# A one-core hybrid backbone (retention, then gMLP): sums of weight quarters recorded one item ahead, and one product moved to another PSUM tag

## The chip, the cores and the metric

The kernel runs on one core of a Trainium2 chip. The metric is the device time of one execution in microseconds (us), lower is better. Engines by the names of the profile: PE (TensorE, the matmuls), PEld (its weight loads), DVE (VectorE), ACT (ScalarE), POOL (GpSimd), SP (SyncE, which here issues most of the DMA loads).

## The reference

Two layers over 512 latent tokens of width 1024, with 256 context tokens ahead of them. Layer 0 mixes tokens by bidirectional multi-scale retention, layer 1 by a chunked gMLP. Cut to what matters here:

```python
for i in range(DEPTH):                                   # 2 layers
    shift_x, scale_x, gate_x = jnp.split(silu_c @ ada_w[i] + ada_b[i], 3, axis=-1)
    hx = rmsnorm(x, norm_g[i]) * (1 + scale_x[:, None]) + shift_x[:, None]
    ...
    if kind == 0:   # q, k, v, z = hx @ w_in (and hc for the context), retention, @ w_out
        out_x, out_c = retention_mixer(hx, hc, ret_w_in[j], ret_decay[j], ret_w_out[j], need_ctx)
    elif kind == 1: # u, v, z = hx @ w_in, norm of v, mix within chunks of 128 tokens, gate, @ w_out
        out_x = gmlp_chunk_mixer(hx, gm_w_in[j], gm_vnorm_g[j], gm_w_s[j], gm_b_s[j], gm_w_out[j])
    x = x + gate_x[:, None] * out_x
return rmsnorm(x, final_g)
```

All data are 32-bit floats. `rmsnorm` needs one inverse root for each token.

## The kernel before

**Products of quarters.** A product with a weight matrix is made quad by quad: a quad is a 2 x 2 block of the weights, with raw quarters 11, 12, 21, 22, each 128 x 1024 numbers in an SBUF slot. Instead of eight quarter products it makes seven, on sums of quarters and of activations (lines 150 to 153): T1 = 12 − 11, T2 = 22 − T1's sum, T3 = 22 − 12, T4 = 21 − T2's sum, each formed in place of a raw quarter, beside the plain B11, B21, B22. The activations' counterparts are A11, A12, A22 and S1 to S4 (in the profile oA and oS). `PAIRED` and `SINGLE` give the order of the seven.

**Halves.** TensorE multiplies numbers of reduced mantissa here, so every operand is split into a high and a low half, and a product is three matmuls (`mm3`, line 125). `split` (line 132) does it for the weights: ACT casts the item to its high half, then DVE subtracts that from the item to get the low half. Both lie in one `hl` tile; four hl tiles rotate. So an item costs ACT a cast, and DVE a low half and, for a T item, a sum ahead of it.

**The stream.** Class `Stream` (line 155) holds the list of items, in the order in which TensorE takes them. `get` returns the next item's tile and calls `upto`, which keeps two items ahead: for each it records the sum (T items; for the last weights a product with the gate in its place), then `split`, then gives the raw slots back (`drop`), after which `pump` issues the next loads on SP.

**Banks.** PSUM has eight banks here: six of tag "ps", two of tag "tm" (`pt`, line 121). Class `Product` (line 329) takes x from "ps" (B11, T2, T3 and T4 accumulate there) and y and z from "tm". ACT copies a bank to SBUF (`snap`), DVE adds a bank to such a copy (`plus`, in the profile `snap<-pst,snap`); T4 goes on in bank x after DVE's plus for T3 has read it.

**Layer 1's norm.** At the end of layer 0 `by_tokens` transposes the residual stream into banks, ACT squares and sums them there, and `residual` (line 1099) copies the same banks to `xs` tiles on ACT, which POOL's queue spills to DRAM. `inverse` forms the inverse roots, `rms` (line 1113) spreads them over the partitions by a product with the unit matrix, two matmuls into a bank, which ACT copies to `rs`. `second_half` (line 1147) is called step by step between the first products of layer 1 and makes the S and A operands from rs.

**Order.** TensorE's instructions stay in the order in which they are recorded. Those of ACT and DVE (and with them the loads on SP and spills on POOL) are put in order by a scheduler when the kernel is built; after that the order on each engine is fixed. It works from the order of recording and from its own estimates of what is ready. All instructions are recorded through one helper, so the profile has line 54 for each.

Of the kernel before, what the change touches and what calls it, by code (L numbers as in the profile page):

```python
# [10 lines left out]
ALU = mybir.AluOpType  # L11
AX = mybir.AxisListType

P = 128
# [12 lines left out]
HS = 256  # L27
# [40 lines left out]
def hybrid_kernel(ctx, tc, xT_d, cT_d, cv_d, sv_d, rows_d, ada0_d, adag_d, w_d, rope_d, dec_d, ws_d, id_d, out_d):  # L68
    nc = tc.nc
    pe, act, dve, sp = (Queue(tc, e) for e in (nc.tensor, nc.scalar, nc.vector, nc.sync))  # L70
# [11 lines left out]
    def st(shape, tag, dt=F32, bufs=1, name=None):  # L82
        return sb.tile(shape, dt, tag=tag, name=name or tag, bufs=bufs)
# [26 lines left out]
    def hl_tile(moves=False):  # L110

        i = hls[0] % HL
        hls[0] += 1
        t = st([P, 2080], f"hl{i}", F32R, name="hl")
        o = 32 if moves != (i % 2 == 1) else 0
        return t[:, o:o + 2048].rearrange("p (a n) -> p a n", a=2)
# [4 lines left out]
    def pt(shape=(P, 512), tag="ps"):  # L121
        return ps.tile(list(shape), F32, tag=tag, name="pst", bufs=6 if tag == "ps" else 2)
# [9 lines left out]
    def split(hl, src, late=None):  # L132
        h, l = hl
        act.copy(h, src)
        low = lambda: dve.tensor_tensor(l, src, f32(h), ALU.subtract)
        if late is None:
            low()
        else:
            late.append(low)
# [15 lines left out]
    class Stream:  # L155
# [3 lines left out]
        def __init__(self):  # L159
            self.items, self.loads, self.raws, self.left, self.tiles = [], [], {}, {}, {}  # L160
            self.free, self.stage, self.done, self.sent, self.at = [], 0, 0, 0, -1
            self.gate = self.limit = self.cap = None

        def quad(self, q, names, place=None):
            for name in names:
                self.item(q, name, place)
# [28 lines left out]
        def upto(self, n, late=None):  # L195

            while self.done < min(n, self.limit or len(self.items)):
                q, name, uses, at, place = self.items[self.done]
                self.pump()
                raw = lambda u: self.raws[q, u]  # L200
                r = raw(at)
                if name[0] == "T":
                    dve.tensor_tensor(r, raw(uses[0]), raw(uses[1]), ALU.subtract)
                elif name[0] == "gated":
                    g = self.gate[:, name[1]:name[1] + 512].unsqueeze(1).to_broadcast([P, 2, 512])
                    rr = r.rearrange("p (e n) -> p e n", e=2)
                    dve.tensor_tensor(rr, rr, g, ALU.mult)
                hl = place() if place else hl_tile(q[0] in ("vz", "v1"))
                split((hl[:, 0, :], hl[:, 1, :]), r, late)
                self.tiles[self.done] = hl  # L210
                self.done += 1
                if late is None:
                    self.drop(q, uses)
                else:
                    late.append(lambda: self.drop(q, uses))

        def drop(self, q, uses):
            for u in uses:
                e = self.left[q, u]
                e[1] -= 1  # L220
                if not e[1]:
                    self.free.append(e[0])
            self.pump()
# [349 lines left out]
    def project(q):  # L573
        if q[0] == "kq":
            return Product(features, kq_done(q[1]), hc)
        return Product(tokens, vz_done(q[1], q[2]), hc)
# [349 lines left out]
    for n, q in enumerate(QUADS[3:]):  # L926
        pr = project(q)
# [183 lines left out]
        dve.reciprocal(s[:, 1, :], s[:, 1, :])  # L1111

    def rms(hf):
        pr = pt((P, HS))
        for i in range(2):
            mm(pr[:, i * P:i * P + P], sums[hf][:, 1, i:i + 1].to_broadcast([P, P]), ident, start=True, stop=True)
        rs = st([P, HS], "rs1", name="rs1")
        act.copy(rs, pr)
        return rs.unsqueeze(1).to_broadcast([P, 4, HS])
# [7 lines left out]
    def first_half(hf, c):  # L1127
        if hf == 0:
            if c == 3:
                by_tokens(0, 0)  # L1130
            return
        if c == 0:
            by_tokens(0, 1)
            inverse(0)
        if c == 2:
            residual()
        if c == 3:
            by_tokens(1, 0)
        if c != 1:
            return  # L1140
        rb = rms(0)
        for g, q in ((0, "11"), (1, "12")):
            op("A" + q)
            scaled(quarter[q], 0, g, rb)
            keep("A" + q, quarter[q])

    def second_half():
        f11, f12, f21, v = (quarter[q] for q in ("11", "12", "21", "22"))
        by_tokens(1, 1)
        inverse(1)  # L1150
        yield
        rb = rms(1)
        dve.tensor_tensor(v, v, rb, ALU.mult)
        op("S1")
        for k in range(4):
            act.activation(A["S1"][:, 0, k, :], v[:, k, :], AF.Identity, bias=shs[:, k:k + 1])
            dve.scalar_tensor_tensor(A["S1"][:, 1, k, :], v[:, k, :], shs[:, k:k + 1], f32(A["S1"][:, 0, k, :]), ALU.add, ALU.subtract)
        yield
        for k in range(4):
            dve.scalar_tensor_tensor(v[:, k, :], v[:, k, :], shs[:, k:k + 1], f11[:, k, :], ALU.add, ALU.subtract)  # L1160
        op("S2")
        keep("S2", v)
        yield
        dve.tensor_tensor(f12, f12, v, ALU.subtract)
        op("S4")
        keep("S4", f12)
        scaled(f21, 1, 0, rb)
        yield
        dve.tensor_tensor(f21, f11, f21, ALU.subtract)
        op("S3")  # L1170
        keep("S3", f21)
        yield
        scaled(f11, 1, 1, rb)
        op("A22")
        keep("A22", f11)
        yield
# [302 lines left out]
```

## Time and profile before

| | us |
|---|---|
| times of three runs | 898.55, 896.89, 896.98 |
| median | 896.98 |
| profiled execution, its own time | 898.68 |
| span of the profiled execution | 896.9 |
| PE busy | 881.9 (98%) |
| DVE busy | 712.7 (79%) |
| ACT busy | 461.2 (51%) |
| POOL busy | 51.5 (6%) |
| DVE, 195 low halves | 236.9, 1.22 each |
| DVE, 92 sums of quarters | 111.5, 1.22 each |
| ACT, 195 casts | 203.6, 1.05 each |

Times within the execution count from the start of the span. Busy times of PE overlap by the pipelining of its matmuls, so a busy share of PE says only that it did not stand idle.

### The profile page before, as it was taken

How to read it: one execution, taken by the hardware profiler on the slowest of the kernel's cores; microseconds unless marked ns; L12 is line 12 of the kernel's file. 1: busy time of each engine (PE TensorE's matmuls, PEld its weight loads, DVE VectorE, ACT ScalarE, POOL GpSimd, SP SyncE). 2: the span in 40 equal slices, each digit the busy share in tenths (PEclk: the TensorE clock that was granted, in tenths of full speed). 3: DMA queues.
4: the chain of work that ended last, by engine and by line, in shares of the span. 5: the costliest groups of instructions: out<-in, count | busy, mean ns of one | idle time of the engine just before them, and what ended most of it. 6: DMA issues, size and time to landing. Idle time of an engine off the chain costs nothing.

```text
span 896.9 us, 16938 instructions
## 1 busy us (share of the span) xinstructions
PE 881.9 (98%) x6884; PEld 839.2 (94%) x6884; DVE 712.7 (79%) x996; ACT 461.2 (51%) x717; POOL 51.5 (6%) x88
## 2 busy tenths in 40 slices
PE   8999999999999999999999999999999999999997
PEld 7899999999999999998989999999999899899986
DVE  2689967699679877877678568999888578688995
ACT  5464644444355534636365438744666446356434
POOL 0001211001101101000000001010000000000000
PEclk9999999999999999999999999999999999999999
DMA  9933968457477448747445421545334235136212
GB/s 334 403 126 107 301 216 260 142 177 242 144 251 239 145 160 329 267 137 253 147 130 176 142 70 62 183 165 192 130 119 166 69 118 179 33 118 211 75 44 94
DMA packets 75486, 153.81 MB, mean 171 GB/s; under 512 B 7696, under 2 KB 34448, under 8 KB 75408
## 3 DMA queue, kind: packets, MB, share of 16 engines
q1 hardware_dynamic: 68544, 130.69, 44.0%
q0 software_dynamic: 6720, 22.03, 6.5%
q8 instruction: 54, 0.88, 0.4%
q14 instruction: 24, 0.20, 0.1%
q10 hardware_dynamic: 144, 0.01, 0.0%
HBM read 128.58 MB, written 24.12 MB: 170 GB/s over the span
## 4 chain that ended last, share of the span: by engine, by line
PE 88%; DVE 5%; ACT 3%; DMA 2%; issue 1%; SPq 1%; DVEq 0%; ACTq 0%
PE pst L54 88%; DVE hl L54 2%; DMA xq<-in_xT_dram 1%; DVE raw L54 1%; DMA raw<-in_w_dram 1%; ACT hl L54 1%; ACT junk L54 1%; SPq L54 1%; ACT f L54 1%; ACT oA L54 0%; DVE ada_a L54 0%; DVE pf L54 0%; DVE pl L54 0%; DVE o L54 0%; DVE f L54 0%
## 5 line engine op out<-in xcount | busy, mean ns | idle before, releaser
L54 DVE TENSOR_TENSOR hl<-raw,hl 128x1024 fp32r<-128x1024 f32 x195 | 236.9, 1222 | 79.4 <-ACT hl L54 79.2
L54 ACT CAST hl<-raw 128x1024 fp32r<-128x1024 f32 x195 | 203.6, 1050 | 140.0 <-PE pst L54 68.9
L54 PE MATMUL pst<-hl,oS 128*128 128x256 f32 x1152 | 138.6, 282 | 2.1 <-DVE hl L54 1.9
L54 PEld LDWEIGHTS pst<-hl,oS 128*128 128x128 f32 x1152 | 136.6, 190 | 3.4 <-DVE hl L54 2.1
L54 PE MATMUL pst<-oS,hl 128*128 128x256 f32 x1104 | 133.6, 280 | 0.7 <-ACT oS L54 0.5
L54 PEld LDWEIGHTS pst<-oS,hl 128*128 128x128 f32 x1104 | 130.2, 189 | 2.3 <-ACT oS L54 1.0
L54 PE MATMUL pst<-oA,hl 128*128 128x256 f32 x936 | 117.4, 281 | 0.2
L54 PEld LDWEIGHTS pst<-oA,hl 128*128 128x128 f32 x936 | 112.0, 189 | 2.5 <-issue 1.2
L54 DVE TENSOR_TENSOR raw<-raw 128x1024 f32<-128x1024 f32 x92 | 111.5, 1219 | 1.4 <-DMA raw<-in_w_dram 0.7
L54 ACT COPY snap<-pst 128x512 f32<-128x512 f32 x92 | 53.8, 585 | 104.1 <-PE pst L54 103.7
L54 PE MATMUL pst<-hl,oA 128*128 128x256 f32 x816 | 99.3, 280 | 0.0
L54 PEld LDWEIGHTS pst<-hl,oA 128*128 128x128 f32 x816 | 97.2, 189 | 0.1
L54 PE MATMUL pst<-og,hl 128*128 128x256 f32 x768 | 92.5, 281 | 0.0
L54 PEld LDWEIGHTS pst<-og,hl 128*128 128x128 f32 x768 | 90.4, 189 | 0.9 <-issue 0.2
L54 PE MATMUL pst<-v,ph 128*128 128x512 f32 x192 | 60.1, 395 | 0.0
L54 PE MATMUL pst<-hl,ya 128*128 128x512 f32 (+1 forms) x246 | 59.2, 386 | 0.0
L54 PEld LDWEIGHTS pst<-hl,ya 128*128 128x128 f32 x246 | 45.3, 188 | 9.5
L54 DVE TENSOR_TENSOR snap<-pst,snap 128x512 f32<-128x512 f32 x69 | 47.3, 686 | 5.3 <-PE pst L54 5.1
L54 ACT CAST ph<-pf 128x512 fp32r<-128x512 f32 x24 | 14.9, 621 | 67.3 <-DVE pf L54 66.9
L54 PE MATMUL pst<-hl,hc 128*128 128x256 f32 x384 | 47.1, 279 | 0.0
L54 PEld LDWEIGHTS pst<-hl,hc 128*128 128x128 f32 x384 | 45.6, 189 | 0.0
L54 PEld LDWEIGHTS pst<-v,ph 128*128 128x128 f32 x192 | 36.2, 188 | 7.3
(177 smaller groups left out, 1003.2 us busy)
## 6 DMA issues: line engine op xcount, KB each, us to landing
raw<-in_w_dram SPq DMA_DIRECT2D x224, 256.0 KB, 3.9
bg<-in_adag_dram SPq DMA_DIRECT2D x32, 512.0 KB, 4.3
ada_w<-in_ada_dram SPq DMA_DIRECT2D x16, 512.0 KB, 8.9
raw<-in_w_dram SPq DMA_DIRECT2D x16, 512.0 KB, 4.4
bg<-in_dec_dram SPq DMA_DIRECT2D x12, 512.0 KB, 4.3
v<-snap POOLq DMA_DIRECT2D x16, 256.0 KB, 4.9
z<-snap POOLq DMA_DIRECT2D x16, 256.0 KB, 3.8
v<-v SPq DMA_DIRECT2D x8, 512.0 KB, 4.2
```

The lines of the kernel that those rows point to most:

```text
L54: made = op(*args, **kw)
```

## The change

Two edits. The first takes the code that forms an item's sum out of `upto` into a method `sum`, which notes in `summed` that it was done. `upto` calls it for an item ahead of its split, as before, and after its loop once more, for the next item, if that item's raw quarters are loaded and it does not lie past the limit. So the sum of an item is recorded one item earlier than its split. The second edit takes the bank of `rms` from tag "tm" instead of "ps". Both kernels have the same instructions on every engine, in TensorE's case in the same order.

```diff
@@ upto
-                raw = lambda u: self.raws[q, u]
-                r = raw(at)
-                if name[0] == "T":
-                    dve.tensor_tensor(r, raw(uses[0]), raw(uses[1]), ALU.subtract)
-                elif name[0] == "gated":
-                    g = self.gate[:, name[1]:name[1] + 512].unsqueeze(1).to_broadcast([P, 2, 512])
-                    rr = r.rearrange("p (e n) -> p e n", e=2)
-                    dve.tensor_tensor(rr, rr, g, ALU.mult)
+                r = self.raws[q, at]
+                self.sum(self.done)
                 hl = place() if place else hl_tile(q[0] in ("vz", "v1"))
                 split((hl[:, 0, :], hl[:, 1, :]), r, late)
...
+            if self.limit is None or self.done < self.limit:
+                self.sum(self.done)
+
+        def sum(self, n):
+
+            if n >= len(self.items) or n in self.summed:
+                return
+            q, name, uses, at, place = self.items[n]
+            if name[0] not in ("T", "gated") or any((q, u) not in self.raws for u in uses):
+                return
+            self.summed.add(n)
...
@@ rms
-        pr = pt((P, HS))
+        pr = pt((P, HS), tag="tm")
```

**Where the order moves (1).** DVE in layer 0, the quad vz 2, 1 (about us 211 to 224 of the span). raw_2239 is quarter 11, later the sums of T1 and then T2; raw_2306 quarter 12, later T3; raw_2309 is 22, raw_2505 is 21, later T4. hl_2682 is T1's tile, hl_2716 T2's, hl_2772 B21's, hl_2803 T3's; a row hl<-raw,hl is a low half. Before:

```order
L54 TENSOR_TENSOR snap_2532<-pst_2464,snap_2532 128x512
L54 TENSOR_TENSOR rope_a_2671<-rope_a_2671,rope_b_2672 128x256 x2
L54 TENSOR_SCALAR ada_a_2299<-bg_2601,cpad_177,ada_a_2299 128x1024
L54 TENSOR_TENSOR raw_2239<-raw_2306,raw_2239 128x1024
L54 TENSOR_TENSOR raw_2306<-raw_2309,raw_2306 128x1024
L54 TENSOR_TENSOR hl_2772<-raw_2505,hl_2772 128x1024
L54 TENSOR_TENSOR hl_2682<-raw_2239,hl_2682 128x1024
L54 TENSOR_SCALAR ada_a_2299<-bg_2678,cpad_177,ada_a_2299 128x1024
L54 TENSOR_TENSOR raw_2239<-raw_2309,raw_2239 128x1024
L54 TENSOR_TENSOR hl_2803<-raw_2306,hl_2803 128x1024
L54 TENSOR_TENSOR raw_2505<-raw_2505,raw_2239 128x1024
L54 TENSOR_TENSOR hl_2716<-raw_2239,hl_2716 128x1024
```

The same place of the changed kernel (numbers of tiles that aren't quarters or hl shift by one):

```order
L54 TENSOR_TENSOR raw_2239<-raw_2306,raw_2239 128x1024
L54 TENSOR_TENSOR snap_2532<-pst_2465,snap_2532 128x512
L54 TENSOR_TENSOR rope_a_2672<-rope_a_2672,rope_b_2673 128x256 x2
L54 TENSOR_SCALAR ada_a_2300<-bg_2602,cpad_177,ada_a_2300 128x1024
L54 TENSOR_TENSOR hl_2682<-raw_2239,hl_2682 128x1024
L54 TENSOR_TENSOR hl_2772<-raw_2505,hl_2772 128x1024
L54 TENSOR_TENSOR raw_2239<-raw_2309,raw_2239 128x1024
L54 TENSOR_SCALAR ada_a_2300<-bg_2679,cpad_177,ada_a_2300 128x1024
L54 TENSOR_TENSOR hl_2716<-raw_2239,hl_2716 128x1024
```

T1's sum has moved ahead of the bank's drain, T2's low half follows its sum with one operation between, and T3's sum and low half and T4's sum, which stood ahead of T2's low half, come later.

**Where the order moves (2).** ACT at the start of layer 1 (about us 557 to 561). pst_6588 (6589 in the changed kernel) is the bank of `rms`. Before:

```order
L54 COPY snap_6586<-pst_6561 128x512
L54 COPY xs_6676<-pst_6471 128x512
L54 COPY xs_6679<-pst_6478 128x512
L54 COPY xs_6682<-pst_6543 128x512
L54 COPY rs1_6591<-pst_6588 128x256
L54 COPY xs_6685<-pst_6550 128x512
```

Now:

```order
L54 COPY snap_6587<-pst_6562 128x512
L54 COPY rs1_6592<-pst_6589 128x256
L54 COPY xs_6677<-pst_6472 128x512
L54 COPY xs_6680<-pst_6479 128x512
L54 COPY xs_6683<-pst_6544 128x512
L54 ACTIVATE oS1_6595<-f22_6141,shs_911,oS1_6595 128x256 x4
```

The copy of the inverse roots now stands ahead of three of the residual's copies instead of behind them.

**Where the order moves (3).** DVE in the same stage. The first two products of layer 1 run side by side (q = 0 and 1); raw_6218 becomes T4's sum of the one, raw_6221 of the other, raw_6212 and raw_6215 hold the T2 sums, hl_6906 and hl_6944 are T4's tiles of the two. Before, about us 556 to 562:

```order
L54 TENSOR_TENSOR raw_6212<-raw_6230,raw_6212 128x1024
L54 RECIPROCAL sums_6137<-sums_6137 128x2
L54 TENSOR_TENSOR raw_6215<-raw_6233,raw_6215 128x1024
L54 TENSOR_TENSOR raw_6218<-raw_6218,raw_6212 128x1024
L54 TENSOR_TENSOR raw_6221<-raw_6221,raw_6215 128x1024
L54 TENSOR_TENSOR f22_6141<-f22_6141,rs1_6591 128x1024
L54 TENSOR_TENSOR f21_6140<-acc_4217,rs1_6591 128x1024
```

In the changed kernel the two T4 sums stand some 25 rows later, shortly ahead of the low halves that need them:

```order
L54 BN_STATS bns_6516<-snap_6786 128x6 x2
L54 TENSOR_TENSOR raw_6218<-raw_6218,raw_6212 128x1024
L54 TENSOR_TENSOR oA22_6865<-f11_6138,oA22_6865 128x1024
L54 TENSOR_TENSOR snap_6820<-pst_6732,snap_6820 128x512
L54 TENSOR_TENSOR hl_6906<-raw_6218,hl_6906 128x1024
L54 BN_STATS bns_6516<-snap_6820 128x6 x2
L54 TENSOR_TENSOR raw_6221<-raw_6221,raw_6215 128x1024
L54 TENSOR_TENSOR snap_6718<-pst_6517,snap_6718 128x512
L54 TENSOR_TENSOR snap_6757<-pst_6562,snap_6757 128x512
L54 BN_STATS bns_6516<-snap_6718 128x6 x2
L54 TENSOR_TENSOR hl_6944<-raw_6221,hl_6944 128x1024
```

Ahead of the `snap` rows that drain a bank by DVE, the same operations stand as before, in another order: the sums have moved to the end of that stretch.

More of the change, by code (lines that the diff above doesn't have):

```diff
@@ L162, in __init__ @@
             self.gate = self.limit = self.cap = None
+            self.summed = set()
         def quad(self, q, names, place=None):
@@ L215, in upto @@
                     late.append(lambda: self.drop(q, uses))
+            if self.limit is None or self.done < self.limit:
[7 more added lines that the diff above has]
+            self.summed.add(n)
+            raw = lambda u: self.raws[q, u]
+            r = raw(at)
+            if name[0] == "gated":
+                g = self.gate[:, name[1]:name[1] + 512].unsqueeze(1).to_broadcast([P, 2, 512])
+                rr = r.rearrange("p (e n) -> p e n", e=2)
+                dve.tensor_tensor(rr, rr, g, ALU.mult)
+            else:
+                dve.tensor_tensor(r, raw(uses[0]), raw(uses[1]), ALU.subtract)
         def drop(self, q, uses):
```

## The prediction

> **What bounds the kernel now.** I read the page first (busy times, then the chain that ended last), then the waits of TensorE, then the two stretches that these waits point to.
>
> ```profile
> span 896.9 us, 16938 instructions
> PE 881.9 (98%) x6884; PEld 839.2 (94%) x6884; DVE 712.7 (79%) x996; ACT 461.2 (51%) x717; POOL 51.5 (6%) x88
> PE 88%; DVE 5%; ACT 3%; DMA 2%; issue 1%; SPq 1%; DVEq 0%; ACTq 0%
> ```
>
> TensorE is busy 98% of the span and carries 88% of the chain. 896.9 − 881.9 = 15.0 us is all that it stands idle, so no edit that only shifts work of other engines can be worth more, except through the pace of the matmuls themselves. Of the waits (total us, times, longest), these can be touched by the change:
>
> ```profile
> PE pst L54 <- DVE hl L54: 1.9, 1, 1.9
> PE pst L54 <- DVE pl L54: 1.2, 2, 0.7
> PE pst L54 <- ACT xs L54: 1.2, 1, 1.2
> ```
>
> One wait for a low half (hl) and one for a bank that still holds data for a copy (xs). The two for pl are in the attention, which the change leaves in its order. The rest of the list is start-up.
>
> **Place 1, us 218 to 231: what the wait for hl costs.** Runs of TensorE's matmuls (start, length):
>
> ```profile
> 216.16 2.88 PE L54 MATMUL pst<-hl,hc 128*128 128x256 f32 x24
> 218.88 3.12 PE L54 MATMUL pst<-hl,oS 128*128 128x256 f32 x25
> 223.94 4.21 PE L54 MATMUL pst<-hl,oS 128*128 128x256 f32 x23 [1.94 <-DVE hl L54]
> 227.95 3.30 PE L54 MATMUL pst<-hl,oA 128*128 128x256 f32 x24
> 231.09 1.10 PE L54 MATMUL pst<-hl,hc 128*128 128x256 f32 x8
> ```
>
> A group of 24 takes 218.88 − 216.16 = 2.72 us undisturbed. The groups of T1 and T2 take 227.95 − 218.88 = 9.07 instead of 5.44 us, the next one 231.09 − 227.95 = 3.14: **3.63 + 0.42 = 4.05 us lost**, though the wait is listed with 1.9. Of it, 2.2 is the stall (25 matmuls should have lasted until 221.7, the next starts at 223.94), 1.4 the 23 matmuls that follow (4.01 us for 2.61) and 0.4 the next group. The clock says why, in windows (length, PE busy, matmuls, clock, DMA share, GB/s):
>
> ```profile
> 196.00:220.00 24.00, 24.00 (x214) 1.00 0.79 256
> 225.00:229.00 4.00, 4.00 (x24) 0.57 0.82 248
> ```
>
> Right behind the stall the granted clock is 0.57, with TensorE busy all the while.
>
> **What the change does there.** VectorE's rows:
>
> ```profile
> 210.92 0.69 DVE L54 TENSOR_TENSOR snap<-pst,snap 128x512 f32<-128x512 f32 x1 [0.30 <-PE pst L54]
> 211.53 0.75 DVE L54 TENSOR_TENSOR rope_a<-rope_a,rope_b 128x256 f32<-128x256 f32 x2
> 212.20 1.28 DVE L54 SCALAR_TENSOR_TENSOR ada_a<-bg,cpad,ada_a 128x1024 f32<-128x1024 f32 x1
> 213.40 2.48 DVE L54 TENSOR_TENSOR raw<-raw 128x1024 f32<-128x1024 f32 x2
> 215.80 2.35 DVE L54 TENSOR_TENSOR hl<-raw,hl 128x1024 fp32r<-128x1024 f32 x2
> ...
> 219.26 1.22 DVE L54 TENSOR_TENSOR raw<-raw 128x1024 f32<-128x1024 f32 x1
> ...
> 222.67 1.22 DVE L54 TENSOR_TENSOR hl<-raw,hl 128x1024 fp32r<-128x1024 f32 x1
> ```
>
> T2's sum is the row at 219.26, and T2's low half the last: it ends at 223.89, and TensorE goes on at 223.94. Between 213.40 and 223.9 VectorE has no gap, so what decides is the order. It has three moves: T1's sum goes ahead of the drain at 210.92, into the 0.30 us that VectorE idles there; T3's sum (the second of the 2.48 row) goes behind; and so do T3's low half and T4's sum, which stood between T2's sum and its low half (the rows left out behind 219.26). One 1024-wide operation is 1.22 us long and the next starts some 1.14 after it (two of them take 2.35). Counted by hand from 210.6: T1's sum to 211.7, drain 0.6, rope 0.67, ada 1.2 to 214.1, two low halves to 216.4, T2's sum to 217.55, ada to 218.75. The cast lies on ScalarE, between its copies:
>
> ```profile
> 220.51 1.05 ACT L54 CAST hl<-raw 128x1024 fp32r<-128x1024 f32 x1 [0.33 <-DVE raw L54]
> ```
>
> It waited for T2's sum before, so it starts at 217.6 to 217.7 now and ends at 218.7; the low half runs 218.75 to 219.95 instead of 222.67 to 223.89. TensorE asks for it at 221.7, so **the stall goes with 1.75 us to spare**. What is late next: T3's low half, which ended at 221.6 and now ends about 225.7; its group stands behind those at 227.95 and 231.09, so not before 231.09 + 2.72 − 4.05 = 229.8: 4 us to spare. The drain at 210.92 is 0.8 later; its bank is next written a group (2.72) or more behind. If that cover were gone, it would cost 0.8. SP's loads into the freed quarters follow the low halves, at most 4 us later, for data used from 242 on.
>
> The half clock I charge to the stall, since it follows within 2 us of it and nowhere else in the stages of full load. So place 1 is −4.05.
>
> A rule of the Trainium skill would have it otherwise. "TensorE: Matmul & The Clock Gate", Part 1, says that the array's clock halves only after a whole idle window of some 3.4 us, on a window that runs free. The row 225 to 229 shows the clock at 0.57 after an idle time of 1.94, so by itself this stall was too short for the rule. If the rule holds and something else halved the clock, the gain would be the 2.2 us of the stall, 898.68 − 2.2 = 896.5.
>
> **Place 2, us 553 to 588: the bank of the inverse roots.** On TensorE:
>
> ```profile
> 558.27 0.71 PE L54 MATMUL pst<-ident,sums 128*128 128x128 f32 x4 [1.16 <-ACT xs L54]
> 587.51 5.70 PE L54 MATMUL pst<-hl,oA 128*128 128x256 f32 x47
> ```
>
> On ScalarE:
>
> ```profile
> 557.63 1.57 ACT L54 COPY xs<-pst 128x512 f32<-128x512 f32 x3
> 559.06 0.41 ACT L54 COPY rs<-pst 128x256 f32<-128x256 f32 x1
> ```
>
> The product waits 1.16 us until the first xs copy has emptied a bank; with small waits next to it I put 1.3 to 1.5 (TensorE's idle time in the window below is 33.91 − 32.61 = 1.30). For a bank of the scores it needs no copy, since what used them is long done. So TensorE is that much further from 558 on, and rs is copied ahead of the three xs (0.5 us each). But on VectorE:
>
> ```profile
> 556.79 3.48 DVE L54 TENSOR_TENSOR raw<-raw 128x1024 f32<-128x1024 f32 x3
> 585.38 1.22 DVE L54 TENSOR_TENSOR oA<-f,oA 128x1024 fp32r<-128x1024 f32 x1
> 586.51 0.69 DVE L54 TENSOR_TENSOR snap<-pst,snap 128x512 f32<-128x512 f32 x1
> 587.11 1.23 DVE L54 TENSOR_TENSOR hl<-raw,hl 128x1024 fp32r<-128x1024 f32 x1
> 553.29:587.20 33.91, 32.61 (x275) 32.17 (x274) 33.90 (x45) 26.25 (x43) 4.30 (x8) 1.00 0.47 156
> ```
>
> The window gives busy time of PE, PEld, DVE, ACT, POOL: VectorE 33.90 of 33.91 us. Here **VectorE is the bound**, and TensorE runs a few tenths behind it. The drain at 586.51 reads the bank into which T4's group then accumulates: it ends at 587.20, T4's first matmul starts at 587.51. The new order takes two of the three sums at 556.79 (2.28 us, T4's) to places behind 580; they are still ahead of that drain, and so is everything else that was. Nothing leaves the stretch. VectorE could only lose: f22 must wait for rs, copied about 558.1, some 0.2 us after the one sum left ahead of it. So the drain ends between 587.1 and 587.4 in before's time, and T4's group starts 0.15 earlier to 0.25 later than now. I take 0: **the 1.3 to 1.5 us won at 558 are a new wait of as much at 586**. The low half of that item, at 587.11 before, is now ready about 589.8 and needed a group later, at 590.2. If it came late, that would be up to 0.5.
>
> **The other moved places** have cover. In the fourth key quad the low half of this row of VectorE goes 1.14 later, to 303.4; TensorE's row starts two groups, and the second, that uses it, begins about 304.3:
>
> ```profile
> 301.02 1.22 DVE L54 TENSOR_TENSOR hl<-raw,hl 128x1024 fp32r<-128x1024 f32 x1
> 301.42 4.86 PE L54 MATMUL pst<-oS,hl 128*128 128x256 f32 x39
> ```
>
> It keeps 0.9. In the last u quad (829 to 848) a sum goes ahead of nine drains, which are 1.14 later each and keep at least 1.7; at 599 to 612 a low half gets earlier. These are 0; all covers lost would be 1.14 at most at each.
>
> **Sum.** The profiled execution took 898.68, 1.78 more than its span. 898.68 − 4.05 + 0 = 894.6, in round numbers **894.5**. The other runs are 898.55, 896.98 and 896.89, so they come in two heights, 1.6 apart, and the profiled one is of the upper. The half clock with its group (1.4 + 0.4 = 1.8) has the size of that step: my guess is that the lower runs have the stall without it. From the median 896.98 the stall alone, 2.2 to 2.5, leads to 894.5 to 894.8 as well; if the median has the whole 4.05 in it, to 892.9. The two agree well enough for one forecast.
>
> **Rivals.** (B) *Faster by the pace.* The same kind of matmul runs at two paces. In windows as above:
>
> ```profile
> 269.00:291.00 22.00, 22.00 (x196) 1.00 0.74 238
> 318.00:347.00 29.00, 29.00 (x257) 1.00 0.68 237
> 590.00:646.00 56.00, 56.00 (x478) 1.00 0.45 154
> 646.00:672.00 26.00, 26.00 (x231) 1.00 0.38 122
> 719.00:740.00 21.00, 21.00 (x187) 1.00 0.37 126
> 784.00:806.00 22.00, 22.00 (x195) 1.00 0.37 121
> 838.00:854.00 16.00, 16.00 (x144) 1.00 0.41 140
> ```
>
> A window counts some 2.5 matmuls of its edges as well; without them 590 to 646 has 475.5 in 56 us, 8.49 per us, the six others 1195 in 136 us, 8.79 per us, 3.5% more, all at clock 1.00. The pace changes at breaks in the stream (behind the stall at 222 the group took 3.14 instead of 2.72). A new break at 586 can tip 590 to 646 into the fast pace: 56 − 475.5/8.79 = 1.9 less, **892.6**. For it: the place is where the break is. Against: it may tip either way. It also holds the case that both waits are really gone (1.5 less, 893.0).
>
> (C) *The half clock stays or comes back*: it wasn't the stall that caused it, or the new wait of 1.5 at 586, close to the 1.94 that preceded it, brings another half clock. 894.5 + 1.8 = **896.3**. The first of the two is what the rule of the Trainium skill above would give. Against: the wait of 1.16 at 558 left the clock at 1.00 (the window of 553 to 587).
>
> (D) *It doesn't do what it says*: the sum comes earlier, but the low half stays behind something else, say the cast behind ScalarE's copies. Then nothing changes: **897 to 898.7**. Against: ScalarE waited 0.33 for the sum.
>
> (E) *Slower by the pace.* The breaks are set anew, and stretches that run fast fall into the slow pace. The six fast windows are 136 us; all of them slow cost 136 × 3.5% = 4.7: 894.5 + 4.7 = **899.2**. It decides from some 4.3, nine tenths of them; against it, their breaks of before (the attention between them) all stay.
>
> **How the numbers follow.** Chances: forecast 0.60, B 0.15, C 0.14, D 0.05, E 0.06. About 0.2% (1.8 us) is what a measurement of this kernel tells from no change, so faster is below 895.2, slower above 898.8. Faster: B and 0.50 of the forecast's 0.60 (its spread, 0.25 at 586 and 0.5 behind, with the two heights of the runs, leaves a tenth above 895.2), 0.65. Same: the rest of it, C and D, 0.29. Slower: E, 0.06. The range goes from a little under B, 892.3, to a little over C, 896.9; D, E and a little of B stay out.
>
> **What would show it.** No wait for DVE hl about 222, and the clock at 1.00 from 220 to 234. No wait for ACT xs, rs copied before the xs. A new wait of TensorE of 1.3 to 1.5 us on VectorE's snap just ahead of T4's group, about 583.4 (587.5 − 4.1), with VectorE still without a gap in the 34 us ahead. Wrong would be: a half clock in the same window without a stall (C), no new wait and T4's group near 582 (then VectorE wasn't the bound), or counts per us of the fast windows down to 8.5 (E).

## The result, and the profile after

The changed kernel took 894.22 us (median of 8 runs, 892.67 to 895.25) against 897.24 us (8 runs, 896.75 to 898.61): ratio 0.9968, 95% interval 0.9959 to 0.9978. The profiled execution took 895.05, its span 893.3. The forecast was 894.5. Measured twice more (e0 and e8 below) the same kernel came to 0.9959 and 0.9985. All three intervals lie below 1, so the gain is clear of noise, and its size is 0.15 to 0.4%.

The waits of TensorE in the changed kernel (total us, times, longest), its first two rows:

```profile
PE pst L54 <- DVE snap L54: 2.7, 1, 2.7
PE pst L54 <- DVE pl L54: 1.5, 3, 0.7
```

The waits for hl (1.9) and for xs (1.2) are gone. At the top stands a new one, for the drain that the prediction named, and it is 2.7 and not 1.3 to 1.5.

**Place 1 after.** TensorE's matmuls, then the clock in windows (length, PE busy, matmuls, clock, DMA share, GB/s):

```profile
216.24 2.99 PE L54 MATMUL pst<-hl,hc 128*128 128x256 f32 x24
219.06 5.82 PE L54 MATMUL pst<-hl,oS 128*128 128x256 f32 x48
224.72 2.99 PE L54 MATMUL pst<-hl,oA 128*128 128x256 f32 x24
227.54 2.99 PE L54 MATMUL pst<-hl,hc 128*128 128x256 f32 x24
```

```profile
220.00:225.00 5.00, 5.00 (x45) 1.00 0.64 211
225.00:229.00 4.00, 4.00 (x36) 1.00 0.90 283
```

The groups of T1 and T2 are one unbroken run of 48, 224.72 − 219.06 = 5.66 us (9.07 before), and the clock stays at 1.00 where it was 0.57. The next group takes 2.82 (3.14 before). That is 3.7 us together; forecast 4.05. The difference is the pace: a group takes 2.82 here and took 2.72 ahead of the stall before. VectorE's and ScalarE's rows:

```profile
216.32 1.22 DVE L54 TENSOR_TENSOR raw<-raw 128x1024 f32<-128x1024 f32 x1
217.46 1.28 DVE L54 SCALAR_TENSOR_TENSOR ada_a<-bg,cpad,ada_a 128x1024 f32<-128x1024 f32 x1
218.67 1.23 DVE L54 TENSOR_TENSOR hl<-raw,hl 128x1024 fp32r<-128x1024 f32 x1
```

```profile
217.58 1.05 ACT L54 CAST hl<-raw 128x1024 fp32r<-128x1024 f32 x1 [0.55 <-DVE raw L54]
```

T2's low half starts at 218.67; counted by hand it was 218.75.

**Place 2 after.** TensorE:

```profile
553.29 0.70 PE L54 MATMUL pst<-ident,sums 128*128 128x128 f32 x4
559.29 21.92 PE L54 MATMUL pst<-hl,oS 128*128 128x256 f32 x192
583.88 8.33 PE L54 MATMUL pst<-hl,oA 128*128 128x256 f32 x57 [2.67 <-DVE snap L54]
```

The row of before that answers to the second:

```profile
564.77 22.90 PE L54 MATMUL pst<-hl,oS 128*128 128x256 f32 x192
```

Read as differences: the product of the inverse roots starts 558.27 − 553.29 = 4.98 earlier, the span ends 3.6 earlier, and T4's group starts 587.51 − 583.88 = 3.63 earlier. So all that place 2 had won ahead of T4's group was given back there. The 192 matmuls took 21.92 instead of 22.90: the stretch ran in the faster pace, TensorE came another microsecond early, and waited longer. VectorE's rows around the drain, and where its unbroken stretch starts:

```profile
549.66 2.36 DVE L54 TENSOR_TENSOR hl<-raw,hl 128x1024 fp32r<-128x1024 f32 x2 [0.69 <-ACT hl L54]
...
581.93 1.20 DVE L54 TENSOR_TENSOR raw<-raw 128x1024 f32<-128x1024 f32 x1
583.05 1.28 DVE L54 TENSOR_TENSOR snap<-pst,snap 128x512 f32<-128x512 f32 x2
```

The first of the two snaps, 0.68 long, ends at 583.73, 34.07 us behind the start; before it was 587.20 − 553.30 = 33.90. Right ahead of it stands a T4 sum (581.93).

**Behind T4's group.** Windows of the changed kernel:

```profile
580.00:590.00 10.00, 7.33 (x50) 0.83 0.89 268
590.00:600.00 10.00, 10.00 (x91) 1.00 0.37 126
600.00:610.00 10.00, 10.00 (x91) 1.00 0.15 54
```

The half clock came back, at 0.83 over the ten microseconds that hold the wait; then the same matmuls ran at 91 in 10 us, where they ran at 87 or 88 before:

```profile
590.00:600.00 10.00, 10.00 (x88) 1.00 0.53 173
600.00:610.00 10.00, 10.00 (x87) 1.00 0.15 54
```

By the starts of all 6884 matmuls against those of before, the half clock cost 1.56 us (lead 3.63 at T4's first matmul, 2.07 at us 589), and the pace gave 1.56 back until about us 640, where the lead is 3.63 again and stays so to the end. So the other moved places gave nothing, as forecast. Two rivals of the prediction, B (for part of its stretch, up to us 628) and C, both happened, and cancelled.

### The profile page after: what moved, and what is told of

Read it like the earlier page. It is cut to its first block, busy times and chain, and to the rows that moved or that the text cites. A ratio compares the mean times of both kernels' runs of the same rounds, so it can differ in the third digit from the quotient of the medians.

```text
span 893.3 us, 16943 instructions
## 1 busy us (share of the span) xinstructions
PE 878.2 (98%) x6884; PEld 835.9 (94%) x6884; DVE 712.8 (80%) x996; ACT 461.9 (52%) x717; POOL 51.5 (6%) x88
## 4 chain that ended last, share of the span: by engine, by line
PE 86%; DVE 7%; ACT 3%; DMA 2%; issue 1%; SPq 1%; DVEq 0%; ACTq 0%
PE pst L54 86%; DVE hl L54 2%; DVE f L54 1%; DMA xq<-in_xT_dram 1%; DMA raw<-in_w_dram 1%; ACT junk L54 1%; DVE oS L54 1%; SPq L54 1%; DVE snap L54 0%; ACT hl L54 0%; DVE pf L54 0%; DVE pl L54 0%; DVE o L54 0%; DVE bns L54 0%; ACT L54 0%
## 5 line engine op out<-in xcount | busy, mean ns | idle before, releaser
L54 PE MATMUL pst<-hl,oS 128*128 128x256 f32 x1152 | 135.5, 278 | 0.0
L54 PEld LDWEIGHTS pst<-hl,oS 128*128 128x128 f32 x1152 | 134.0, 188 | 0.8 <-ACT snap L54 0.8
```

The costliest lines, as they stand in the source:

```text
L54: made = op(*args, **kw)
```

## The experiments

Theory A: the gain is place 1 alone, a stall and the half clock behind it; at place 2 VectorE's queue sets when T4's group starts, so that what the bank wins comes back as a wait. The rivals are named with each run. Times are medians; "before" is the kernel before, measured beside them on the same chip (e0 to e3 on one, e4 to e7 on a second, e8 to e11 on a third).

| run | us (runs) | before | ratio, 95% interval | wait ahead of T4's group |
|---|---|---|---|---|
| e0 both parts | 892.93 (7) | 896.38 | 0.9959 (0.9944 to 0.9973) | 1.6 |
| e1 sums only | 893.28 (8) | 896.38 | 0.9963 (0.9949 to 0.9978) | 0.4 |
| e2 bank only | 896.08 (12) | 896.38 | 0.9994 (0.9981 to 1.0007) | 0.5 |
| e3 statistics late | 891.88 (6) | 896.38 | 0.9951 (0.9938 to 0.9965) | none |
| e4 not in layer 1 | 891.21 (6) | 894.61 | 0.9943 (0.9921 to 0.9964) | 0.5 |
| e8 both parts | 894.15 (12) | 896.22 | 0.9985 (0.9972 to 0.9998) | 2.6 |
| e9 as e3 | 889.98 (6) | 896.22 | 0.9934 (0.9912 to 0.9956) | none |
| e10 as e4 | 891.78 (6) | 896.22 | 0.9953 (0.9935 to 0.9972) | 0.5 |
| e11 e3 and e4 | 890.99 (6) | 896.22 | 0.9946 (0.9925 to 0.9967) | none |

e5, e6 and e7 ran once each, on the chip of e4: 897.80, 900.87 and 894.14 us.

### The two parts apart: e0, e1, e2

e0 is the changed kernel.

> The changed kernel unaltered, once more, as the mark for the others and for a second trace of it. Theory A (place 1 alone is worth the gain; at place 2 VectorE is the bound, so that the 1.3 us won at the bank come back as a wait ahead of T4's group): ratio 0.9968, some 894.2 us; a wait of TensorE on VectorE's snap of 1.3 us if the stage runs in the slow pace, 2.7 in the fast one, and T4's group at the same distance from the end of layer 0 in both. Rival B (the gain also rests on the pace of the matmuls): the pace of us 553 to 630 is the same as in the first trace, fast, and T4's wait 2.7.

Here T4's wait is 1.6:

```profile
583.08 9.19 PE L54 MATMUL pst<-hl,oA 128*128 128x256 f32 x76 [1.62 <-DVE snap L54]
```

The starts are 118 ns apart in this stretch (113 in the first trace), and the wait is the shorter one. So the length of the wait follows TensorE's pace, while the start of the group follows VectorE: theory A. Rival B missed: the pace of 553 to 630 isn't a property of the kernel.

e1 leaves the bank as before:

```diff
-        pr = pt((P, HS), tag="tm")
+        pr = pt((P, HS))
```

> Only the sums one item ahead; the product of layer 1's inverse roots keeps its bank of the common tag. Theory A: the same time as both parts, 894.2 +- 0.7; the wait for ACT xs of 1.2 is back at us 554, and the wait on snap ahead of T4's group is smaller by 1.3 or gone. Rival (the bank is worth its 1.3 us by itself, the wait at T4 comes from T4's sums, which the first part moved into that stretch): 1.3 slower than both, 895.5, with the same wait at T4 on top.

```profile
554.84 0.71 PE L54 MATMUL pst<-ident,sums 128*128 128x128 f32 x4 [1.16 <-ACT xs L54]
583.93 8.30 PE L54 MATMUL pst<-hl,oA 128*128 128x256 f32 x71 [0.41 <-DVE snap L54]
```

As theory A has it: the wait for xs is back, the one ahead of T4 is 0.4 instead of 1.6, and the time is that of both parts within the interval. Its order answers a question that the order of the whole change left open. VectorE's rows of e1 at the start of the stretch:

```profile
553.37 3.48 DVE L54 TENSOR_TENSOR raw<-raw 128x1024 f32<-128x1024 f32 x3
556.76 1.22 DVE L54 TENSOR_TENSOR f<-f,rs 128x1024 f32<-128x1024 f32 x1
```

All three sums are still there: the sums ahead don't move T4's two sums. The bank does: with rs ready earlier, the scheduler puts f before them.

e2 is the kernel before with the bank alone (`tag="tm"` in `rms`).

> Only the bank; the sums stand where they stood before, with T4's two sums at the start of layer 1's first stretch. Theory A: no gain, 897.2 +- 0.5: the stall of 1.9 at us 222 with its half clock stays, the wait for xs is gone, and TensorE waits 1.3 or more on VectorE's snap ahead of T4's group. Rival (T4's moved sums make that wait): no wait at T4, and 1.3 to 1.5 faster, 895.8.

```profile
224.06 4.17 PE L54 MATMUL pst<-hl,oS 128*128 128x256 f32 x23 [1.77 <-DVE hl L54]
585.94 3.10 PE L54 MATMUL pst<-hl,oA 128*128 128x256 f32 x25 [0.49 <-DVE snap L54]
589.36 2.90 PE L54 MATMUL pst<-hl,oA 128*128 128x256 f32 x23 [0.33 <-DVE hl L54]
```

The time is as expected, no gain that shows (0.9994), and the stall at 222 stays, with its half clock. But the wait ahead of T4 is 0.5 and not 1.3 or more. Theory A's order was wrong for this kernel:

```profile
585.11 0.69 DVE L54 TENSOR_TENSOR snap<-pst,snap 128x512 f32<-128x512 f32 x1
585.71 1.22 DVE L54 TENSOR_TENSOR raw<-raw 128x1024 f32<-128x1024 f32 x1
```

With the bank alone, the second T4 sum lands behind the drain. VectorE's stretch (from 552.85 to 585.80) is 32.95, one sum shorter. By the trace the bank alone wins 1.1 us of its 1.3 ahead of T4's group (33.09 us from the start of the stretch to the group's start, 34.21 before), and 0.33 of that goes again in the wait for a low half behind it; the interval of the time can't show that. With both parts the sum one ahead brings that T4 sum back in front of the drain, and the 1.1 is lost. The expectation's rival (T4's moved sums make the wait) was half right: one of the two does, and only with both parts.

### VectorE's queue: e3, e4 and again e9, e10, e11

e3 takes work out of the stretch without leaving any out: the statistics of the first two quads are recorded one by one behind T4's group.

```diff
+    late_stats = []
...
-            for t in range(2):
-                dve.bn_stats(bns[:, 2 * th + t, 2 * cb + nh, :], c[:, t * HS:t * HS + HS])
+            stats = lambda: [dve.bn_stats(bns[:, 2 * th + t, 2 * cb + nh, :], c[:, t * HS:t * HS + HS]) for t in range(2)]
+            if cb < 2:
+                late_stats.append(stats)
+            else:
+                stats()
...
+                if late_stats and (a == 2 or name == "T4"):
+                    late_stats.pop(0)()
```

> Both parts, and the statistics (bn_stats) of the first two quads of layer 1 recorded one by one behind T4's group, so that four pairs of them, 4 x 0.66 = 2.6 us of VectorE, leave the stretch that ends with T4's drain. Theory A (VectorE's backlog sets when T4's group starts): the wait of 2.7 shrinks to under 0.3, the half clock behind it goes too (1.4), so 2.7 to 4.1 faster than both: 890.1 to 891.5. Rival (the wait hangs on the chain of the operand A22 or on the matmuls themselves, not on VectorE's queue): the wait stays above 2, 894.2. What may eat the gain: the statistics that now stand among the low halves behind T4.

```profile
578.95 0.69 DVE L54 TENSOR_TENSOR snap<-pst,snap 128x512 f32<-128x512 f32 x1
580.61 11.59 PE L54 MATMUL pst<-hl,oA 128*128 128x256 f32 x97
```

No wait: the drain ends 31.47 us behind the start of VectorE's stretch at 548.17, 2.6 less, as counted, and TensorE comes a microsecond later than the drain. The time is 1.05 below both parts, less than the 2.7 to 4.1 expected, and the intervals overlap. e0's trace has the short wait of 1.6 and no half clock, so there was only 1.6 to win in it; that e0's other executions were like it isn't shown.

e4 keeps both parts, but records no sum ahead in layer 1's first product:

```diff
-            if self.limit is None or self.done < self.limit:
+            if (self.limit is None or self.done < self.limit) and self.done < len(self.items) and self.items[self.done][0][0] != "v1":
                 self.sum(self.done)
```

> Both parts, but in layer 1's first product (v1) the sums are recorded with their splits as before; everywhere else one ahead. In the order this puts the second quad's T4 sum, 1.13 us of VectorE, behind T4's drain instead of ahead of it. Theory A (VectorE's queue ahead of that drain is the wait): the wait ahead of T4's group is shorter by 1.1 at the same pace, 0.5 in the slow pace (1.6 with both parts), 1.6 in the fast one (2.7); the time is 0.5 to 1.1 less than with both parts, with some tenths given back to the low half of the second T4, which is 0.3 late. Rival (sums ahead are worth something in this product too): as with both parts or slower.

```profile
580.15 0.68 DVE L54 TENSOR_TENSOR snap<-pst,snap 128x512 f32<-128x512 f32 x1
580.75 1.22 DVE L54 TENSOR_TENSOR raw<-raw 128x1024 f32<-128x1024 f32 x1
580.98 3.09 PE L54 MATMUL pst<-hl,oA 128*128 128x256 f32 x25 [0.48 <-DVE snap L54]
```

The sum is behind the drain, the wait 0.5, as forecast to the tenth, with VectorE's stretch at 32.94. To compare times with both parts on one chip, e3 and e4 stand once more beside the changed kernel, and beside a kernel with both edits:

> The changed kernel on the same chip as the three below, as their mark: ratio 0.996 to 0.997 to the kernel before. Its profile shows T4's wait of 1.6 (slow pace) or 2.7 (fast pace).

> Both parts with the statistics of layer 1's first two quads behind T4's group, a second time and beside the changed kernel. Theory A: no wait ahead of T4's group, 1.6 to 2.7 less than both, with the half clock's 1.4 less in some executions; ratio to before 0.993 to 0.995. Rival (the wait costs nothing, the matmuls behind it make up for it): as both, 0.996.

> Both parts without the sums one ahead in layer 1's first product, a second time beside the changed kernel. Theory A: waits of 0.5 and 0.3 instead of 1.6 (slow pace), so some 0.8 to 1.1 less than both: 0.995 to 0.996.

> Both edits together: statistics late and no sums ahead in layer 1's first product. Theory A: with the statistics gone VectorE is no longer the bound of the stretch, so the second edit adds nothing: as with the statistics late alone within 0.5 us, 0.993 to 0.995, and no wait ahead of T4. Rival: the two gains add up, another 1.1 less.

Medians: 894.15 (both), 889.98 (statistics late), 891.78 (not in layer 1), 890.99 (the two together). Both variants beat the changed kernel: e9's interval ends at 0.9956, e10's at 0.9972, where that of e8 starts. For e8 the forecast 0.996 to 0.997 missed; it was 0.9985, and the reason is open. e10 came out 2.4 us below e8, more than the 0.8 to 1.1 expected: e8's trace has the long wait of 2.65 and a half clock behind it, e10's no half clock and no wait there above 0.5. TensorE's rows of e8 and e9 ahead of T4's group:

```profile
574.83 4.13 PE L54 MATMUL pst<-hl,oS 128*128 128x256 f32 x35
581.61 8.65 PE L54 MATMUL pst<-hl,oA 128*128 128x256 f32 x60 [2.65 <-DVE snap L54]
```

```profile
574.74 6.17 PE L54 MATMUL pst<-hl,oS 128*128 128x256 f32 x53
580.97 9.23 PE L54 MATMUL pst<-hl,oA 128*128 128x256 f32 x76
```

e11 is no better than e9 (890.99 and 889.98, intervals that overlap), as theory A says: with the statistics gone VectorE isn't the bound there, and the second edit has nothing left to win (in its trace TensorE waits 0.8 at the next drain, about us 621, instead). The lowest median is that of the statistics late in e9 (0.9934; 0.9951 in e3). The intervals of e3, e4, e9, e10 and e11 overlap, so which of these versions is the fastest isn't settled.

### The half clock: e5, e6, e7

e5 and e6 make T2's low half late again, by doing its cast three or four times more on ScalarE (e5 is shown):

```diff
+                if q == ("vz", 2, 1) and name == "T2":
+                    for _ in range(3):
+                        act.copy(hl[:, 0, :], r)
                 split((hl[:, 0, :], hl[:, 1, :]), r, late)
```

> Both parts, with the cast of T2's item of the quad vz 2, 1 done three times more on ScalarE (the same numbers again), so that its low half is late again and TensorE stalls about us 222, by my count of the order 1.4 to 2.2 us. Theory A (a stall of over some 1.7 us brings the half clock, which costs 1.4 more): if the stall comes out at 1.8 or more, the clock falls to 0.5 within 2 us behind it and the quad loses 1.4 on top; if it comes out at 1.6 or less, it stays 1.00. Rival (the half clock hangs on the place, or on an idle window of 3.4 us): 1.00 in both cases.

> The same with four casts more: a stall of 2.2 to 3.2 us at the same place. Theory A: clock 0.5 for some 3 us behind it, 1.4 us lost on top of the stall. Rival: 1.00.

TensorE and the clock in e5:

```profile
222.71 0.38 PE L54 MATMUL pst<-hl,oS 128*128 128x256 f32 x1 [1.06 <-ACT hl L54]
224.16 4.49 PE L54 MATMUL pst<-hl,oS 128*128 128x256 f32 x23 [1.07 <-DVE hl L54]
```

```profile
225.00:228.00 3.00, 3.00 (x17) 0.52 0.88 282
```

And in e6:

```profile
224.15 0.49 PE L54 MATMUL pst<-hl,oS 128*128 128x256 f32 x1 [2.49 <-ACT hl L54]
225.41 5.28 PE L54 MATMUL pst<-hl,oS 128*128 128x256 f32 x23 [0.77 <-DVE hl L54]
```

```profile
225.00:231.00 6.00, 5.59 (x26) 0.50 0.73 231
```

The same matmuls at the same place ran at clock 1.00 with no stall (the changed kernel) and at half clock as soon as they were stalled again, by 2.13 us in two pieces and by 3.26 in two. With the longer stall the half clock is longer too, 6.83 us (224.28 to 231.11) instead of 3.41. So the stall is the cause, and the rival (the place) falls. e6 as a whole is 900.87: one late item, with a half clock behind T4's wait as well, costs the gain and more.

e7 is the changed kernel once more:

> The changed kernel a third time, for the spread of one execution: theory A says that T4's group starts 34 us behind the start of VectorE's unbroken stretch whatever the pace; its wait is 1.6 where the stretch runs in the slow pace and 2.7 in the fast one, and only the longer one is followed by the half clock.

```profile
583.02 9.19 PE L54 MATMUL pst<-hl,oA 128*128 128x256 f32 x76 [2.67 <-DVE snap L54]
```

T4's group starts 34.3 us behind the start of VectorE's stretch (548.75), as expected, and the wait is the long one. But no half clock followed, though the stall is as long as in the first trace. So the length of the stall doesn't decide alone.

Its position does. In every trace the granted clock changes only at times that are whole multiples of 3.413 us apart; the first rise comes at us 4.1 to 6.9, at another time in each execution. Cut into windows by these times, the first trace has 1.46 of 3.41 us busy in the window that holds most of the stall, and the half clock is exactly the next window:

```profile
581.93:585.34 3.41, 1.46 (x13) 1.00 0.86 265
585.34:588.75 3.41, 3.41 (x19) 0.50 0.97 315
```

In e7 the stall lies across two windows, with 1.15 and 1.53 us idle, and the clock stays at 1.00 in the third:

```profile
578.07:581.49 3.42, 2.27 (x21) 1.00 0.91 289
581.49:584.90 3.41, 1.88 (x16) 1.00 0.85 265
584.90:588.31 3.41, 3.41 (x32) 1.00 0.84 295
```

The same count fits all fourteen traces between us 20 and the last matmuls: each fall of the clock came behind a window with 1.77 to 2.65 us idle (before 1.94, first trace 1.95, e2 1.77, e5 2.09, e6 2.49 and 2.38, e8 2.65), and none behind a window with 1.63 or less (e0 1.62, e5's later stall 1.63).

## Why the prediction was right

**Place 1, −4.05 forecast.** Right in mechanism and nearly in size. The order put T2's low half where it was counted, within 0.1 us. The 3.7 of the first trace are short of 4.05 by the pace of its groups (2.82 instead of 2.72); in e0, in the faster pace, the matmul that had been 0.10 late ahead of this place was 4.34 early behind it. One reading of the rows was wrong without harm to the sum: the 3.14 us of the group behind the stall were put down to its pace, but the half clock lasted until 228.62 and held the first three of its matmuls.

**The half clock charged to the stall.** Shown by e5 and e6 at this place. The rule that spoke against it ("TensorE: Matmul & The Clock Gate", Part 1: The HAM clock gate, of the Trainium skill: an idle window of some 3.4 us) does not hold as a length of idle time: stalls of 1.77 (e2), 1.94 (before) and 1.06 + 1.07 (e5) halved the clock. Its other half, that the window runs free, agrees with the fourteen traces: the clock changes on a grid of 3.41 us that starts at another time in each execution, and a window about half idle (1.77 us or more) was enough.

**Place 2, 0 forecast.** The sum was right, and the place and the reason: T4's group starts a fixed 34.1 to 34.3 us behind the start of VectorE's stretch, in before, e0, e1, e7, e8 and the first trace, whatever TensorE does. The term that was mis-sized is the new wait: "1.3 to 1.5" was 2.6 or 2.7 in three of the four traces of this kernel with the sums and the bank (first, e7, e8) and 1.6 in e0. What failed is the step that TensorE keeps its pace in this stretch. The prediction weighed the pace for 590 to 646 only. It missed, too, that the bank by itself would have kept 1.1 of its 1.3 up to T4's group, and that the first part takes that away: it worked out the whole change, and never asked which part moves T4's sums.

**The rivals.** B and C, at 0.15 and 0.14, were treated as exclusive. In the first trace both happened, the half clock as C had it, behind the new wait, and the pace as B had it, up to us 628; 1.56 up, 1.56 down. That the sum of three terms met the forecast there is in part luck. So is the base: the 4.05 was taken from the profiled execution, 898.68, which is above all eight runs of before; their median, 897.24, moved by 3.0 and not by 4.05. For a median run the prediction had two answers, 894.5 with the stall alone and 892.9 with the half clock in it, and the measured 894.2 lies between them. In e8, with the half clock and the faster pace again, the ratio is 0.9985. D and E did not happen.

**The two heights of before.** The guess that its lower runs lack the half clock was not tried; it stays open. It is possible: with the stall anywhere in the windows above, 1.94 us of stall puts 1.77 or more into one window at 53% of the positions, and more than 1.63 at 61% (an estimate, all positions taken as equally likely). But the later runs of before spread wider than two heights, by 3.7 to 5.8 us on each chip (892.97 to 898.77 on the third).

## What to carry to other kernels

Ahead of a drain on an engine that never rests, a wait removed on TensorE can come back at the drain, as the 1.3 us did here; count that engine's operations between the start of its unbroken stretch and the drain, and take something out of that stretch (here the statistics, which are not read before all quads are done) rather than a wait out of TensorE. When a change has two parts and a scheduler decides the order, look at the order of each part alone: here the bank alone won 1.1 us by its trace, and the other part undid that. Here a wait listed with 1.94 us cost some 4, through the clock behind it.

## What the runs showed of the hardware

The matmuls of 256 columns run at two steady paces, all at clock 1.00: starts 113.3 ns apart, or 117.8 ns. Most stretches keep their pace in all fourteen traces (60 to 167 slow, about 272 to 289 fast), but 189 to 229 and 549 to 645 took either, in executions of the same kernel: 549 to 645 was slow throughout in e0, and in e8 it was fast from 553 to 579 and from 585 to 626 and slow from there on. In the profile of before, some 3700 matmuls ran slow, about 17 us in all against the faster pace. What sets the pace was not found, and its 17 us are more than anything that this change moves.

The half clock lasted 3.41 us each time, and twice that in e6. In it the starts are 213 ns apart, and a single one cost 1.5 to 1.7 us against the pace around it. It followed single stalls of 1.77, 1.94, 2.65, 2.67 and 2.68 us, and did not follow one of 2.67 (e7), those of 1.62 and 1.63 and two of 1.16. What told them apart is the idle time within one window of 3.41 us: 1.77 or more, or 1.63 or less.
